# A hybrid encoder step on one core: handlers, squares and the last norm moved to other places

## Chip, core and metric

One core of a Trainium2 chip runs the kernel. The metric is the device time of one execution in microseconds (us). Engines are called TensorE (PE in rows; PEld its weight loads), VectorE (DVE), ScalarE (ACT), GpSimd (POOL) and SyncE (SP, which only issues transfers).

## The reference

One inference step of a one-layer encoder trunk, on 512 new frames and 32 frames of a running stream, 544 columns in all, with 2048 channels:

```python
# x: 544 rows of 2048, handled transposed in the kernel
z = rmsnorm(x, g_mix) @ w_in                       # 6152 wide: gb, gc, hin, q, k, v, 8 gates
yc = gb * short_conv(gc * hin)                     # width 3, over time
ya = forgetting_attention(q, k, v, cumsum(log_sigmoid(gates)))      # 8 heads of 128
x += concat(rmsnorm(yc, g_conv_out), rmsnorm(ya, g_attn_out)) @ w_out
x += cross_attention(rmsnorm(x, g_xattn), memory)  # 4 heads, 256 memory tokens
x += square(relu(rmsnorm(x, g_mlp) @ w_up)) @ w_down                # hidden 8192
y = rmsnorm(x, g_final)
```

The new keys, values, gates, last convolution rows and memory keys and values are returned too. All of it is fp32. A matrix product is made of three products of rounded parts: each operand is split into a high and a low half (`split`: ScalarE writes the rounded high half, VectorE subtracts for the low one), and hi x hi, hi x lo and lo x hi are added up in PSUM.

## The kernel before

Everything is channel-major: a tile holds 128 channels by 544 columns, `TH` = 272 being one half of the columns. The program is written in Python against a tile framework, which orders each engine's instructions at build time. It goes by priority, which is the place in the program, and takes at each moment of its own timing model the first instruction that is ready. `tc.high_priority(offset=n)` lifts instructions by n places; weight splits (`operand`) and sums of weight blocks (`combine`) are lifted by `AHEAD` = 40. Each engine and each queue then works in that fixed order. A tile comes from a pool with a number of buffers per tag, and an allocation waits until a buffer is free.

Large products use a seven-product scheme on 2x2 blocks (`class Seven`, run by `seven`): for a pair of 128-channel output tiles, four raw weight blocks a11, a12 (tag "raw", 3 buffers) and a21, a22 (tag "raw2", 4 buffers) are loaded, VectorE forms s1 = a21 + a22, s2 = s1 - a11, s4 = a12 - s2 and s3 = a11 - a21 (tag "sum", 3 buffers), and seven products of 24 matmuls each follow in the order b11, t1, t2, b22, t3, b21, t4. t2 is added onto what b11 left in PSUM, after ScalarE has copied that out (L280). The tags "hi" and "lo" have four buffers of 512 columns each, two products' worth. With `late=2` (first pair of a stage) b11 and t1 do the first six channel blocks, then the last two each. `fetch` loads a pair's blocks, `prefetch` the next pair's. `between` is called after t2.

The stages around the change, in order of time:

- **Head** (to 58 us). For j = 0 to 7, two x tiles are loaded (`xr`, L363) and a block of first weights (L364); ScalarE scales x by the gain (L367), `operands` makes the split operands (kept in `xops`), and 48 matmuls (L378) add to four output tiles hr0, gc0, gb0, hr1. `square` squares each x tile on ScalarE and adds it to `acc_x` on VectorE (L189, L163).
- **First norm and gates.** `rstd` sums the squares over channels by a matmul with 1/D (L178, name ssq), takes Ln and Exp on ScalarE and one Newton step in four VectorE instructions (L181 to L184). It is lifted by 150. `emit_logf` does 80 gate matmuls (L418). The four first tiles are scaled by the norm (L557) and given to their handlers: `on_hr` keeps the tile, `on_gc` forms u = gc * hr and the three-tap convolution (L502 to L512), `on_gb` multiplies by the gate, splits, stores and squares (L518, L88, L189). `evac_logf` scales the gates (z16).
- **Projection pairs** (70 to 540 us). Each pair of tiles goes through `seven`; the first tile's handler runs after b21 (`mid`), the second one's after the pair (`done`); a gb tile as second is held until the next pair's `between` (`release`). A gate step follows each of the first six pairs.
- Attention, output projection and cross-attention (540 to 912 us). In these `tmp` tiles (tag "t", 6 buffers of 548 columns) serve as scratch.
- **The MLP's entry** (912 to 992 us). For 16 tiles in the order 0, 8, 1, 9, ... the output of cross-attention is added to x2 (a `tmp` tile reloaded from DRAM), the sum is stored, squared by ScalarE (L1085) and added to one of two accumulators by a copy that accumulates, issued by POOL (L1086), and made into operands. The squares lie in "raw2" buffers, those of the last pair of tiles in `tmp`. Then come 32 pairs of w_up. The norm is applied after the product (`relu`, needing `rb_3`), and is made in `between` of the first pair.
- Down projection, and at the end (`a` = 0, 1: the halves of the columns) eight blocks of last weights each, the final sums, squares, gain, `rstd`, one multiplication per output pair (`finish`, VectorE) and stores, alternately from ScalarE's and SP's queues. The first half's outputs are finished during the second half.

## Time and profile before

| | us |
|---|---|
| median of 3 runs (2349.14 to 2350.31) | 2350.08 |
| the profiled execution | 2352.74 |
| its span, first to last instruction | 2351.0 |
| TensorE busy in it | 2312.8 |
| VectorE busy | 1999.7 |
| ScalarE busy | 1300.0 |
| POOL busy | 212.2 |

The profile is of one execution. Busy time of TensorE is that of pipelined matmuls, whose ends are modelled. Idle time before an instruction is put down to what released it. Starts are us from the start of the span.

### The profile page before, as it was taken

The page shows a single profiled execution, that of the slowest core. Times are in us where ns is not written, and L with a number is a line of the kernel's source. Part 1 is how long each engine was busy: PE and PEld are TensorE (multiplying, and loading weights), DVE is VectorE, ACT ScalarE, POOL GpSimd, SP SyncE. Part 2 cuts the span into 40 slices and gives each one's busy share as a digit, 9 for nine tenths or more (in the row PEclk, how much of TensorE's full clock was granted, in tenths as well). Part 3 has the DMA queues.
Part 4 walks back from the last instruction along what each step waited for, and adds up shares of the span by engine and source line. Part 5 has one row for each costly group of instructions (what it writes and reads, how often), then busy time and mean ns, then how long its engine had stood idle before and what let it go on. Part 6 is the DMA issues. An engine that isn't in the chain of part 4 may idle for free.

```text
span 2351.0 us, 47516 instructions
## 1 busy us (share of the span) xinstructions
PE 2312.8 (98%) x18151; PEld 2285.0 (97%) x18151; DVE 1999.7 (85%) x3546; ACT 1300.0 (55%) x2524; POOL 212.2 (9%) x402
## 2 busy tenths in 40 slices
PE   8999999999999999899999999999999999999997
PEld 8999999999999998799999999999999999999997
DVE  9999988877767757889999999998598888888887
ACT  8455555555644546556666566665255555555555
POOL 0000011114200001111111111111000000000000
PEclk9999999999999999999999999999999999999999
DMA  5333345578435537656565566556946636645523
GB/s 177 127 121 122 122 156 160 160 243 300 141 100 154 157 107 212 200 162 204 191 199 180 193 201 196 188 185 226 344 148 241 211 125 233 228 141 191 184 90 131
DMA packets 161861, 420.25 MB, mean 179 GB/s; under 512 B 19096, under 2 KB 23888, under 8 KB 161632
## 3 DMA queue, kind: packets, MB, share of 16 engines
q1 hardware_dynamic: 109888, 313.54, 39.8%
q0 software_dynamic: 46240, 94.75, 13.1%
q10 hardware_dynamic: 5504, 8.93, 1.1%
q8 instruction: 142, 2.33, 0.4%
q14 instruction: 87, 0.71, 0.1%
HBM read 319.91 MB, written 93.33 MB: 176 GB/s over the span
## 4 chain that ended last, share of the span: by engine, by line
PE 94%; DMA 2%; DVE 2%; ACT 1%; issue 1%; DVEq 0%; ACTq 0%; SPq 0%; POOLq 0%
PE mmx L271 27%; PE dx L1233 14%; PE mmy L271 14%; PE mm L120 13%; PE mm L1233 11%; PE mmz L271 7%; PE mm L1327 2%; PE mm L378 1%; PE h L378 1%; PE mm L914 1%; PE s L644 1%; DMA acc<-sq 1%; DMA raw<-in_w_ends 1%; DVE wlo L85 1%; DMA f<-fd 1%
## 5 line engine op out<-in xcount | busy, mean ns | idle before, releaser
L84 ACT ACTIVATE whi<-raw 128x512 fp32r<-128x512 f32 x664 | 417.8, 631 | 493.9 <-PE mmx L271 97.9
L84 ACT ACTIVATE whi<-sum 128x512 fp32r<-128x512 f32 x652 | 407.5, 630 | 418.6 <-PE mmx L271 186.2
L85 DVE TENSOR_TENSOR wlo<-raw,whi 128x512 fp32r<-128x512 f32 x664 | 453.3, 687 | 129.2 <-ACT whi L84 121.6
L85 DVE TENSOR_TENSOR wlo<-sum,whi 128x512 fp32r<-128x512 f32 x652 | 436.7, 684 | 70.3 <-ACT whi L84 65.9
L271 PE MATMUL mmx<-oph,whi 128*128 128x272 f32 x1296 | 372.8, 288 | 2.3 <-ACT h L280 2.2
L271 PE MATMUL mmx<-oph,wlo 128*128 128x272 f32 x1296 | 374.0, 289 | 0.1
L271 PE MATMUL mmx<-opl,whi 128*128 128x272 f32 x1296 | 371.5, 287 | 0.0
L1233 PE MATMUL dx<-f,whi 128*128 128x272 f32 x1792 | 344.4, 288 | 0.0
L1233 PEld LDWEIGHTS dx<-f,whi 128*128 128x128 f32 x1792 | 281.5, 188 | 0.0
L1233 PE MATMUL mm<-f,whi 128*128 128x272 f32 x1344 | 258.6, 288 | 0.0
L1233 PE MATMUL dx<-f,wlo 128*128 128x272 f32 x896 | 258.4, 288 | 0.0
L271 PE MATMUL mmy<-oph,whi 128*128 128x272 f32 x864 | 249.8, 289 | 7.6 <-ACT whi L84 7.6
L271 PE MATMUL mmy<-oph,wlo 128*128 128x272 f32 x864 | 249.9, 289 | 0.0
L271 PE MATMUL mmy<-opl,whi 128*128 128x272 f32 x864 | 248.9, 288 | 0.0
L271 PEld LDWEIGHTS mmx<-oph,whi 128*128 128x128 f32 x1296 | 244.0, 188 | 3.1 <-ACT h L280 2.6
L271 PEld LDWEIGHTS mmx<-oph,wlo 128*128 128x128 f32 x1296 | 243.3, 188 | 0.5 <-DVE wlo L85 0.5
L271 PEld LDWEIGHTS mmx<-opl,whi 128*128 128x128 f32 x1296 | 243.5, 188 | 0.0
L1233 PEld LDWEIGHTS mm<-f,whi 128*128 128x128 f32 x1344 | 210.6, 188 | 0.0
L1233 PE MATMUL mm<-f,wlo 128*128 128x272 f32 x672 | 193.4, 288 | 0.0
L271 PEld LDWEIGHTS mmy<-oph,whi 128*128 128x128 f32 x864 | 163.4, 189 | 8.1 <-ACT whi L84 8.0
L1233 PEld LDWEIGHTS dx<-f,wlo 128*128 128x128 f32 x896 | 168.9, 189 | 0.0
L271 PE MATMUL mmx<-b,whi 128*128 128x272 f32 x864 | 166.1, 289 | 0.1
(393 smaller groups left out, 5161.5 us busy)
## 6 DMA issues: line engine op xcount, KB each, us to landing
raw<-in_w_up SPq DMA_DIRECT2D x128, 512.0 KB, 3.9
raw<-in_w_dn SPq DMA_DIRECT2D x112, 512.0 KB, 4.4
f<-fd SPq DMA_DIRECT2D x196, 272.0 KB, 5.7
fd<-form POOLq DMA_DIRECT2D x168, 272.0 KB, 4.2
raw<-in_w_in SPq DMA_DIRECT2D x88, 512.0 KB, 3.8
raw<-in_w_out SPq DMA_DIRECT2D x32, 512.0 KB, 4.2
raw<-in_w_ends SPq DMA_DIRECT2D x20, 512.0 KB, 4.2
kq<-hl POOLq DMA_DIRECT2D x32, 256.0 KB, 3.3
```

The source lines that it names most:

```text
L84: act.activation(hi, src, AF.Copy)
L85: dve.tensor_tensor(lo, src, hi.bitcast(F32), ALU.subtract)
L120: pe.matmul(ps[a], w, two(x)[:, a], start=first and n == 0, stop=last and n == 2)
L271: pe.matmul(ps, a[:, c], x, start=first and j == 0 and n == 0, stop=j == 7 and n == 2, skip_group_check=not first)
L378: pe.matmul(ps[a], w[:, c], xs[a][q], start=j + i == 0 and n == 0, stop=j + i == 8 and n == 2)
L644: pe.matmul(s[:, :N], q[a][:, c], k[b][:, :N], start=n == 0, stop=n == 2)
L914: pe.matmul(ps[:, 0, :NMEM], w[:, c], x, start=k == 0 and n == 0, stop=k == KD - 1 and n == 2)
L1233: pe.matmul(ps, a[:, c], f[:, x], start=first and j == 0 and n == 0, stop=j == 3 and n == 2, skip_group_check=not first)
L1327: pe.matmul(ps, w[:, c], two(x)[:, a], start=k == 0 and j == 0, stop=k == 3 and j == 2)
```

## The change

Five things are done.

1. The head asks for the first weight block ahead of the first two x tiles, loads the gate weights `wf` at once on ScalarE's queue, and scales the first x tile on VectorE instead of ScalarE. From the second step on the squares of x are added by accumulating copies from POOL's queue into two accumulators; the first step's squares are written there by ScalarE.
2. The first norm and the four handlers (`begin`) are called in `between` of the first pair instead of ahead of it; `rstd` is no longer lifted, and takes an output tile. The gate steps come one pair later. The last gb tile is held for the next pair like the others.
3. The scratch pool has seven buffers instead of six. It now also holds `wf_hl`, the sample attention's `Ps` and `PTs`, and `xsP`.
4. At the MLP's entry the squares of the last three pairs of tiles (j > 4), instead of the last one, lie in the scratch pool, and `rb_3` is made after b22 (`behind`) instead of after t2.
5. The final norm (`last_rstd`) takes the last square without adding it to the accumulator first, as a second matmul, uses three dependent VectorE instructions instead of four after Exp, and leaves its result in PSUM. For the second half, POOL multiplies three of the eight output pairs, from a copy in SBUF; for the first half the norm is made one block later.

```diff
-    tpool = ctx.enter_context(tc.tile_pool(name="tmp", bufs=6))
+    tpool = ctx.enter_context(tc.tile_pool(name="tmp", bufs=7))
-    def rstd(acc, dim, width=T, early=0):
+    def rstd(acc, dim, width=T, out=None):
         accs = acc if isinstance(acc, list) else [acc]
-        with tc.high_priority(offset=early):
-            rt = npool.tile([128, T], F32, tag="rstd", name="rstd", bufs=3)
+        with tc.high_priority(offset=0):
+            rt = out if out is not None else npool.tile([128, T], F32, tag="rstd", name="rstd", bufs=3)
...
-    def seven(pl, ops, ws, out, scale, mid, prefetch, between=None, late=0):
+    def seven(pl, ops, ws, out, scale, mid, prefetch, between=None, late=0, behind=None):
...
         s.b22()
+        if behind:
+            behind()
         s.t3()
...
-    acc_x = new_acc()
+    acc_x = [new_acc(), new_acc()]
...
+    wf = headp.tile([128, KD, 8], F32, name="wf")
+    act.dma_start(wf, w_f)
...
         xr = [headp.tile([128, T], F32, tag="xr", name="xr", bufs=5) for i in range(2)]
+        if j == 0:
+            hi, lo = weights(w_first[j])
         for i in range(2):
             sp.dma_start(xr[i], xT[j + 8 * i])
-        hi, lo = weights(w_first[j])
+        if j:
+            hi, lo = weights(w_first[j])
...
-            act.activation(x[:, 2 * i:2 * i + 2], two(xr[i]), AF.Identity, scale=gain(G_MIX, j + 8 * i))
+            if j + i == 0:
+                dve.tensor_scalar(x[:, :2], two(xr[i]), gain(G_MIX, 0), None, ALU.mult)
+            else:
+                act.activation(x[:, 2 * i:2 * i + 2], two(xr[i]), AF.Identity, scale=gain(G_MIX, j + 8 * i))
...
-            square(xr[i], acc_x, j + i == 0)
+            if j:
+                sq = tmp("sq")[:, :T]
+                act.activation(sq, xr[i], AF.Square)
+                pool.dma_start(acc_x[i], sq, accum_op=ALU.add)
+            else:
+                act.activation(acc_x[i], xr[i], AF.Square)
...
-    rb = rstd(acc_x, D, early=150)
+    rb = npool.tile([128, T], F32, tag="rstd", name="rb", bufs=3)
     rbs = npool.tile([128, T], F32, tag="rstd", name="rbs", bufs=3)
-    dve.tensor_scalar(rbs, rb, SCALE, None, ALU.mult)
...
+    def begin():
+        rstd(acc_x, D, out=rb)
+        for t, (n, j) in enumerate((("hr", 0), ("gc", 0), ("gb", 0), ("hr", 1))):
+            dve.tensor_tensor(first_tiles[t], first_tiles[t], rb, ALU.mult)
+            kinds[n][1](j, first_tiles[t])
+        box["z"] = evac_logf(ps)
+        dve.tensor_scalar(rbs, rb, SCALE, None, ALU.mult)
...
-        nxt = seven(pj, xops, nxt, out, scale, mid, ahead, release, 2 if i == 0 else 0)
+        nxt = seven(pj, xops, nxt, out, scale, mid, ahead, release if i else begin, 0 if i else 2)
         done(i, out[1])
-        if i < len(steps):
-            steps[i]()
+        if 1 <= i <= len(steps):
+            steps[i - 1]()
         if pairs[i][1] == ("gb", 7):
-            release()
-            keep_cm.__exit__(None, None, None)
...
-        st.P = P = rp.tile([128, LS], F32, tag="Ps", name="Ps")
+        st.P = P = tmp("Ps")[:, :LS]
...
-            sq = (tmp("sq") if j == 7 else up.tile([128, 1024], F32, tag="raw2", name="sq", bufs=4))[:, :T]
+            sq = (tmp("sq") if j > 4 else up.tile([128, 1024], F32, tag="raw2", name="sq", bufs=4))[:, :T]
...
-                    lambda: fetch_up(i + 1), (lambda: rb_3.append(rstd(acc_3, D))) if i == 0 else None,
-                    2 if i == 0 else 0)
+                    lambda: fetch_up(i + 1), None, 2 if i == 0 else 0,
+                    (lambda: rb_3.append(rstd(acc_3, D))) if i == 0 else None)
...
+    def last_rstd(accs):
+        ps = aux("ssq")[:, :TH]
+        for n, t in enumerate(accs):
+            pe.matmul(ps, inv[D], t, start=n == 0, stop=n == len(accs) - 1)
...
+        act.activation(r0, ps, AF.Ln, bias=eps)
+        dve.tensor_scalar(v, ps, EPS, -0.5, ALU.add, ALU.mult)
+        act.activation(r0, r0, AF.Exp, scale=-0.5)
+        dve.tensor_tensor(q, r0, r0, ALU.mult)
+        dve.tensor_tensor(q, q, v, ALU.mult)
+        r = aux("r")[:, :TH]
+        dve.scalar_tensor_tensor(r, q, 1.5, r0, ALU.add, ALU.mult)
+        return r
...
-        rb_4 = rstd(acc_4, D, TH)
+        sums = [acc_4[:, :TH], sq_4]
+    rb_4 = last_rstd(sums)
+    rb_5 = tmp("rb")[:, :TH]
+    act.activation(rb_5, rb_4, AF.Copy)
     for p in range(8):
-        store(p, 1, finish((1, p), rb_4))
+        store(p, 1, finish((1, p), rb_5 if p in (2, 4, 7) else rb_4, pool if p in (2, 4, 7) else dve))
```

## Rows read from the trace of the kernel before

**Rows 1.** From the page, its first part: busy us of each engine, its share of the span, and the number of instructions.

```profile
PE 2312.8 (98%) x18151; PEld 2285.0 (97%) x18151; DVE 1999.7 (85%) x3546; ACT 1300.0 (55%) x2524; POOL 212.2 (9%) x402
```

**Rows 2.** A table of stretches. Columns: the stretch and its length; busy us and number of instructions of PE, PEld, DVE, ACT and POOL; the clock granted to TensorE as a share of full speed; the busy share of the 16 DMA engines; GB/s.

```profile
7.09:14.57 7.48, 7.48 (x38) 7.32 (x39) 7.43 (x22) 7.06 (x14) 0.00 (x0) 1.00 0.82 309
14.57:58.60 44.03, 44.00 (x346) 43.26 (x345) 43.58 (x82) 38.16 (x74) 0.00 (x0) 1.00 0.45 142
...
69.95:81.20 11.25, 9.76 (x76) 9.36 (x76) 11.25 (x18) 4.82 (x10) 1.22 (x2) 1.00 0.37 120
81.20:102.20 21.00, 21.00 (x165) 20.11 (x163) 19.63 (x38) 10.44 (x19) 0.00 (x0) 1.00 0.32 110
102.20:300.00 197.80, 197.00 (x1569) 196.40 (x1568) 186.16 (x321) 102.04 (x185) 10.04 (x19) 1.00 0.36 119
540.00:700.00 160.00, 159.98 (x1206) 151.02 (x1205) 117.92 (x364) 88.93 (x226) 34.55 (x64) 1.00 0.50 168
...
957.80:964.20 6.40, 0.10 (x2) 0.05 (x1) 1.95 (x3) 0.78 (x3) 1.72 (x2) 0.81 0.88 238
964.20:977.20 13.00, 8.28 (x38) 6.77 (x38) 9.56 (x15) 5.79 (x13) 0.00 (x0) 0.70 0.64 189
977.20:992.20 15.00, 15.00 (x120) 15.00 (x121) 14.18 (x26) 8.24 (x16) 0.00 (x0) 1.00 0.21 72
...
2341.50:2351.00 9.50, 0.00 (x0) 0.00 (x0) 4.41 (x7) 0.00 (x0) 0.00 (x0) 0.50 0.69 235
```

**Rows 3.** The timeline at the start of the span: start, us, engine, line, operation, out<-in, shapes, count, and in brackets the idle time ahead and what ended it.

```profile
1.15 0.30 POOL masks.py:199 TENSOR_SCALAR_AFFINE_SELECT ident<-ident 128x128 f32<-128x128 f32 x1
...
3.82 1.51 ACT L367 ACTIVATE x<-xr,vec 128x544 f32<-128x544 f32 x2 [1.33 <-DMA vec<-in_vecs]
...
7.09 1.50 PE L378 MATMUL mm<-b,whi 128*128 128x272 f32 x5 [7.09 <-ACT whi L84]
...
12.78 0.72 DVE L163 TENSOR_TENSOR acc<-acc,sq 128x544 f32<-128x544 f32 x1
...
13.69 0.65 ACT L189 ACTIVATE sq<-xr 128x544 f32<-128x544 f32 x1
```

**Rows 4.** The chain of work that ended last, in order of time, in the stretch 0 to 130: start, us, what, count.

```profile
58.63 1.16 PE ssq L178 x4
...
60.16 9.79 PE mm L418 x80
...
83.96 3.02 PE mmx L271 x24
```

**Rows 5.** What TensorE waited for between 60 and 540, all of it: us in total, times, longest.

```profile
PE mmx L271 <- ACT h L280: 2.2, 2, 1.5
```

**Rows 6.** VectorE's groups of instructions between 59.9 and 78, shapes kept apart: line, engine, operation, names, shapes, count, then busy us, mean ns of one, and idle us before them.

```profile
L557 DVE TENSOR_TENSOR hr<-hr,rstd 128x544 f32<-128x544 f32 x2 | 1.4, 717 | 0.0
L181 DVE TENSOR_TENSOR nt<-rstd 128x272 f32<-128x272 f32 x2 | 0.8, 439 | 0.8 <-ACT rstd L180 0.8
L511 DVE SCALAR_TENSOR_TENSOR y<-u,vec,y 128x546 f32<-128x546 f32 x1 | 0.8, 781 | 0.0
L88 DVE SCALAR_TENSOR_TENSOR ych<-gb,vec,ych 128x544 fp32r<-128x544 f32 x1 | 0.8, 778 | 0.0
L502 DVE TENSOR_TENSOR u<-gc,hr 128x512 f32<-128x512 f32 x1 | 0.7, 682 | 0.0
L183 DVE TENSOR_SCALAR nt<-nt 128x272 f32<-128x272 f32 x2 | 0.5, 290 | 0.0
L510 DVE TENSOR_SCALAR y<-u,vec 128x546 f32<-128x546 f32 x1 | 0.5, 499 | 0.0
L503 DVE TENSOR_TENSOR u<-gc,hr 128x32 f32<-128x32 f32 x1 | 0.2, 183 | 0.0
```

**Rows 7.** VectorE's timeline in the first pair, a run of low halves (columns as in rows 3).

```profile
77.48 2.48 DVE L85 TENSOR_TENSOR wlo<-sum,whi 128x512 fp32r<-128x512 f32 x4
```

**Rows 8.** The timeline at the MLP's entry, first TensorE's three waits, then VectorE's (columns as in rows 3).

```profile
964.15 0.60 PE L271 MATMUL mmy<-oph,whi 128*128 128x272 f32 x1 [6.30 <-ACT whi L84]
...
968.33 2.18 PE L178 MATMUL ssq<-acc,inv 128*128 128x272 f32 x4 [3.35 <-DMA acc<-sq]
...
977.17 0.39 PE L271 MATMUL mmy<-oph,whi 128*128 128x272 f32 x1 [1.27 <-ACT whi L84]
...
962.15 1.23 DVE L232 TENSOR_TENSOR sum<-raw,raw 128x1024 f32<-128x1024 f32 x1 [5.76 <-DMA raw<-in_w_up]
```

**Rows 9.** Transfers at the MLP's entry. First what SP's queue waited for from 930 to 965 (us in total, times, longest); then POOL's queue from 905 to 985 (packets, MB, share of the 16 engines' time); POOL's issues of accumulating copies (busy us, mean ns of one | idle before); and how long these took from issue to landing.

```profile
SPq L222 <- DMA acc<-sq: 8.2, 3, 6.2
...
q0 software_dynamic: 2016, 3.90, 28.7%
...
L1086 POOL DMA_DIRECT2D acc<-sq x14 | 12.1, 863 | 51.5 <-ACT sq L1085 28.7 <-DMA acc<-sq 13.4 <-ACT oph L84 7.7
...
DMA to landing us min/median/max: 4.0/6.7/8.2
```

**Rows 10.** The chain that ended last, after the last matmul: start, us, what.

```profile
2336.73 0.45 DVE acc L163
...
2337.99 0.50 ACT rstd L179
...
2339.93 0.31 DVE nt L183
```

More of the change, by code (lines that the diff above doesn't have):

```diff
@@ L190, in square @@
         accumulate(acc[:, cols], sq[:, cols], first)
-    wf = cpool.tile([128, KD, 8], F32, name="wf")
-    wf_hl = cpool.tile([128, KD, 16], F32R, name="wf_hl")
     sel16 = cpool.tile([16, 8], F32, name="sel16")
@@ L551, in fetch_pair @@
         return fetch(pj, w_in, *(kinds[n][0] + j for n, j in pairs[i]), last)
-    steps = (lambda: gate_open(z16), gate_exp, gate_log, gate_close, gate_sum, turn_logf)
-    ps = emit_logf()
-    nxt = fetch_pair(0)
-    for t, (n, j) in enumerate((("hr", 0), ("gc", 0), ("gb", 0), ("hr", 1))):
-        dve.tensor_tensor(first_tiles[t], first_tiles[t], rb, ALU.mult)
-        kinds[n][1](j, first_tiles[t])
-    z16 = evac_logf(ps)
     held = []
@@ L564, in release @@
             held.pop()()
+    steps = (lambda: gate_open(box["z"]), gate_exp, gate_log, gate_close, gate_sum, turn_logf)
+    ps = emit_logf()
+    nxt = fetch_pair(0)
+    box = {}
+    def begin():
[5 more added lines that the diff above has]
+        dve.tensor_scalar(rbs, rb, SCALE, None, ALU.mult)
     def job(i):
@@ L732, in samp_transpose @@
         pt = aux("pts")
-        PT = pl.tile([128, 3, 128], F32, tag="PTs", name="PTs")
+        PT = tmp("PTs")[:, :384].rearrange("p (a b) -> p a b", a=3)
         n = L // 128
@@ L1024, in xs_scores @@
         mx = xp.tile([128, 3], F32, name="xsmx")
-        P = xp.tile([128, NMEM], F32, name="xsP")
+        P = tmp("xsP")[:, :NMEM]
         dve.tensor_reduce(mx[:, 0:1], s[:, :NMEM], axis=AX.X, op=ALU.max, negate=True)
@@ L1286, in hybrid_step, with finish @@
     fin = {}
-    def finish(p, r):
+    def finish(p, r, eng):
         y = fin.pop(p)
-        dve.tensor_tensor(two(y), two(y), r[:, :TH].unsqueeze(1).to_broadcast([128, 2, TH]), ALU.mult)
+        eng.tensor_tensor(two(y), two(y), r.unsqueeze(1).to_broadcast([128, 2, TH]), ALU.mult)
         return y
+    def last_rstd(accs):
+        ps = aux("ssq")[:, :TH]
+        for n, t in enumerate(accs):
+            pe.matmul(ps, inv[D], t, start=n == 0, stop=n == len(accs) - 1)
+        r0 = npool.tile([128, T], F32, tag="rstd", name="r0", bufs=3)[:, :TH]
+        v, q = (tmp(n)[:, :TH] for n in ("v", "q"))
+        act.activation(r0, ps, AF.Ln, bias=eps)
[6 more added lines that the diff above has]
+        return r
     def store(p, a, y):
@@ L1329, in hybrid_step @@
                 dve.tensor_tensor(xa, xa, ps, ALU.add)
-                square(xa, acc_4, n == 0 and i == 0, slice(0, TH))
+                if n == 7 and i == 1:
+                    sq_4 = tmp("sq")[:, :TH]
+                    act.activation(sq_4, xa, AF.Square)
+                else:
+                    square(xa, acc_4, n == 0 and i == 0, slice(0, TH))
                 act.activation(two(y)[:, i], xa, AF.Identity, scale=gain(G_FIN, m))
-            if a and n:
-                store(n - 1, 0, finish((0, n - 1), rb_4))
+            if a and n == 0:
+                rb_4 = last_rstd(sums)
+            elif a:
+                store(n - 1, 0, finish((0, n - 1), rb_4, dve))
         if a:
-            store(7, 0, finish((0, 7), rb_4))
-        rb_4 = rstd(acc_4, D, TH)
+            store(7, 0, finish((0, 7), rb_4, dve))
+        sums = [acc_4[:, :TH], sq_4]
+    rb_4 = last_rstd(sums)
+    rb_5 = tmp("rb")[:, :TH]
+    act.activation(rb_5, rb_4, AF.Copy)
     for p in range(8):
-        store(p, 1, finish((1, p), rb_4))
+        store(p, 1, finish((1, p), rb_5 if p in (2, 4, 7) else rb_4, pool if p in (2, 4, 7) else dve))
     down_cm.__exit__(None, None, None)
```

5 lines of the change are left out of this document (3 added, 2 removed).

## The prediction

> **What bounds the kernel now.** I read the page first: TensorE is busy for 98% of the span [rows 1], so a gain can only come from its idle time, 38 us in all. A table of stretches shows where that lies: 7.1 us before its first matmul [rows 3], 1.5 us near 76, 0.8 us between 102 and 300, 6.3 and 4.7 us on either side of 964, and the end of the span [rows 2]. The other thing to see in that table is VectorE: it is busy 11.25 of 11.25 us around the gap at 76 and for 94% of the time up to 300. In the input projection it is the next engine to bind, so what is moved onto it there is soon paid for. Then I read each gap for itself: the timeline at the start [rows 3], the chain around 76 [rows 4], TensorE's waits in the projection [rows 5], the MLP's entry [rows 8, 9] and the end [rows 10].
>
> **First loads reordered.** Today ScalarE scales two x tiles from 3.82 (1.5 us), rounds two halves and the first weights, and TensorE begins at 7.09 [rows 3]. Afterwards the weights are asked for ahead of x, so ScalarE can round them early, and VectorE scales the first x tile (0.50 us, as L510 in [rows 6]). But x then lands behind 0.5 MB more, 1.7 us at 309 GB/s [rows 2]; some of it is hidden, since x has to wait for the gains until 3.8 anyhow. I take x at 5.0, scaled at 5.5, rounded at 6.2, first matmul at 6.4: -0.7 us. Bounds: -1.9 (x as early as now) and +0.3 (ScalarE takes the second x tile ahead of the rounding).
>
> **Head squares by accumulating copies.** VectorE loses 16 additions of 0.72 us [rows 3]. But TensorE ran 346 matmuls in 44.0 us there [rows 2], at 0.126 us each when nothing is late (24 in 3.02 us [rows 4]), so at most 0.5 us is to be had. Against it stand 14 accumulating copies on POOL's queue. At the MLP's entry the same 14 took 28.7% of the 16 DMA engines' time in 80 us, 1.64 us each, and they form chains: issue 0.86, landing 6.7 in the median and 8.2 at most [rows 9]. Two chains of seven links of 7.6 us start at 14.3, the end of the second step's first square [rows 3], and end near 67.5. The sum of squares will be asked for near 77 (75.97 less 1.2 and 0.7, and one product of 3.0). So 9.6 us cover it; seven of the longest links, 9.1, would end at 78. Taken: 0; bounds -0.5 and +11 (a link of 10.5 us, below).
>
> The Trainium skill speaks against this edit: by DMA: Bandwidth & Descriptors, section "Issuing engines are not separate DMA queues", copies issued by POOL run on the same 16 DMA engines as those of SP and ACT, so that a further queue adds no room. By that rule 23 us of accumulating copies come on top of the loads' 20 us (share 0.45 of 44 us), 43 of 44, and links would be long, which is the third rival below. The trace agrees in so far as the share was 0.88 where both kinds ran together [rows 2].
>
> **Two accumulators.** The sum takes eight matmul records where four took 1.16 us [rows 4]: +1.2 us, on TensorE itself.
>
> **First channel tiles' handlers moved behind the third product of the first pair.** Removed: the wait of 1.5 us near 76. ScalarE was busy with handler output and weights while TensorE waited for its copy L280 [rows 5]; without the handlers that copy runs at once: -1.5 us (0 if something else is there).
>
> Moved: one burst of VectorE work. By the durations of [rows 6]: rstd's Newton steps 2 x (3 x 0.44 + 0.29) = 3.2; four scalings and z16, 5 x 0.72 = 3.6; u and the gate product with their 32-column rests 2 x (0.68 + 0.18) = 1.7; four small ones, under 0.18 each, 0.7; the taps 0.50 + 2 x 0.78 = 2.1; a low half 0.8; a copy and rbs, as L510, 1.0. That is 13.1 us in 27 instructions, each starting some 0.08 us before the one ahead ends (four low halves of 0.68 us take 2.48 [rows 7]), so 11.0. It used to run between 60 and 77, where TensorE had 9.8 us of gate matmuls to do [rows 4]. There VectorE will now idle, and it can't work far ahead, since four hi and four lo tiles hold two products.
>
> Let T0 be the end of the third product. TensorE does 2.3 us of sums and then the two products that are already split, 3.0 each: fed until T0 + 8.3. The sixth product's tiles come free from T0 + 3.8 on, but its split stands 58 instructions behind the burst's end and is lifted by 40 only, so VectorE does the burst first. It begins at T0 + 2.2 (first sums 1.2, two ScalarE steps of 0.5 as at the end [rows 10]), ends at T0 + 13.2, and the first low tile takes 0.7 more. TensorE, after two matmuls that need no low tile, waits from T0 + 8.6 to T0 + 13.9, 5.3 us; some of the next pair's sums can be done ahead, so I take **+5**. Bounds: 0 (the split is placed ahead of the handlers) and +11 (nothing absorbed, for VectorE has only 1.4 us idle in the pair that follows [rows 2]). What is late next is the sixth product and all behind it in the pair.
>
> The last gate tile's handler no longer runs at once beside another. Of TensorE's two waits for L280 in the projection, 2.2 us together [rows 5], the second, 0.7, falls there: -0.7 (0 to -0.7).
>
> **The MLP's entry.** TensorE waits 6.30 us for weights, because VectorE's sum of two raw blocks waited 5.76 for a transfer [rows 8], which SP could issue only when copies of squares had freed the raw2 buffers (three waits, 8.2 us [rows 9]). In the new kernel the squares from the sixth pair of tiles on lie in the scratch pool, so raw2 comes free with earlier copies and the blocks can land by 955. Then TensorE waits 3.35 for the accumulating copies, as the norm's sum stands ahead of the second product; it is now placed one product (3.0 us) later. Then 1.27. Together 10.9 us, and some 2 us more, as the granted clock was 0.70 in the mean of that stretch [rows 2].
>
> Not all of it returns. VectorE had no idle time before 956.4 (962.15 less 5.76), and still has to do the raw sum and its low halves (1.2 + 1.3), the last tiles' operands (5 x 0.72 + 3 x 0.44 = 4.9), s2 and its low halves (2.5). So the second product begins near 959 and the third near 966; that one, the fourth, the sums and three more (5 x 3.0 + 2.3) end the pair at 983.5, against 992.2 now (its last 120 matmuls fill the stretch from 977.2 [rows 2]): 8.7. The scratch pool, seven buffers for reloads and six squares, can make a reload 1 to 2 us late. I take **-8**; bounds -12 and -1.
>
> **The end.** The last square's addition (0.45) and one of four Newton steps (0.31) leave the chain [rows 10]: -0.8. One more sum for the first half's norm: +0.3. The stores run at a DMA share of 0.69 over 9.5 us, the fill and the last landing included [rows 2], 8 x 272 KB in a stream; so products shared with POOL gain nothing unless they hold the stream up. No POOL multiply is in this trace: its nearest row, 0.30 us for 128 columns [rows 3], makes 1.3 for 544; VectorE's, 0.72. Together -0.5, bounds -0.8 and +0.4.
>
> The rest (guests in the scratch pool, wf by ScalarE's queue at once, gate steps one pair later) I cost at nothing: in the attention stage TensorE is busy for 159.98 of 160 us [rows 2], and the seventh buffer stands in for the guests. Without that cover a late guest costs TensorE one low half, 0.7.
>
> **Sum.** -0.7 + 0 + 1.2 - 1.5 + 5 - 0.7 - 8 - 0.5 = **-5.2 us**. The profiled execution took 2352.74 us (span 2351.0 and 1.7 around it), 0.11% above the median of the runs, 2350.08. So 2347.5 on its scale and 2344.9 on the median's: **2345 us**.
>
> **The rivals.** First: the burst costs nothing, as the build puts the sixth product's split ahead of the handlers. VectorE's 13 us of idle pieces from 81 to 300 [rows 2] would hold it; against it, those pieces are waits for buffers. -10.2: 2340 us. Second: the entry's wait only changes its name, as the norm's sum is again pulled ahead on TensorE's queue, as before [rows 8], and the copies' chain ends no earlier. Then 2 of the 8 us are gained: 2351 us. Third, slower, by one mechanism: the head's loads and accumulating copies fill the DMA engines. A link over 9.0 us makes TensorE wait at T0 seven times the excess; the gain is gone at 9.7, and at 10.5 the wait is 10.7: 2355.6 us. For it, 8.2 + 0.9 was seen; against it, the median, 7.6.
>
> **How the numbers follow.** My forecast 0.45, the rivals 0.25, 0.2 and 0.1. A measurement of this kernel tells 0.2% (4.7 us) from no change. Faster than 2345.4: the first rival and half of my forecast, 0.48. Within: the other half and most of the second, 0.40. Slower than 2354.8: the third and a remnant, 0.12. The range 2338 to 2353 takes in the first two rivals; left out are the third and the ends where all bounds fall together, 2334 and 2373.
>
> **What would show it.** A first matmul near 6.4, no wait for loads in the head, and the last accumulating copy landed before the sum. No wait near 76, and instead, some 8 us after the third product, about 5 us for a low half with VectorE full. At the entry raw sums before 957, waits under 5 us in place of 10.9, a granted clock near 1. At the end 0.8 us less from last matmul to first store. I am wrong if VectorE shows slack behind the burst, or if the norm's sum still stands ahead of the second product.

## The result, and the profile after

The changed kernel takes 2355.76 us in the median (2353.12 to 2359.58), beside 2351.07 for the kernel before: ratio 1.0019, 95% interval 1.0011 to 1.0027. It is 4.7 us slower (2.6 to 6.3) where 5.2 us less were forecast. Its profiled execution took 2354.01 us with a span of 2352.0; before it was 2352.74 and 2351.0. These two single executions differ by 1.3 us, less than the medians, so below a term is read from a stretch of the trace and checked on the medians of kernels that have one part alone or one part undone. Either reading is good to about 1 us. One execution each of entry_alone, sum_in_old_place, direct_sums and squares_on_vector was 6% to several times longer than its others; ranges and ratios leave it out. In the code after, L271, L280 and L289 are L269, L278 and L287; the head's matmuls are L386, the gate matmuls L430.

The stretches that answer to [rows 2] (same columns, the changed kernel):

```profile
7.09:14.57 7.48, 6.52 (x39) 6.42 (x40) 7.17 (x23) 7.42 (x16) 0.00 (x0) 1.00 0.98 331
14.57:58.60 44.03, 43.46 (x347) 43.24 (x345) 36.86 (x70) 38.81 (x78) 12.26 (x14) 1.00 0.97 238
69.95:81.20 11.25, 11.25 (x85) 10.91 (x85) 7.72 (x10) 6.16 (x13) 0.00 (x0) 1.00 0.10 40
81.20:102.20 21.00, 16.82 (x126) 15.75 (x125) 21.00 (x51) 8.21 (x15) 1.11 (x2) 1.00 0.24 78
...
957.80:964.20 6.40, 2.72 (x19) 2.36 (x17) 3.27 (x6) 3.27 (x6) 0.86 (x1) 0.95 1.06 351
964.20:977.20 13.00, 10.76 (x57) 9.74 (x56) 10.71 (x16) 8.38 (x17) 1.72 (x2) 0.76 0.57 144
977.20:992.20 15.00, 13.75 (x109) 13.75 (x110) 14.50 (x28) 7.60 (x15) 0.00 (x0) 1.00 0.41 139
```

Three things are to be seen. The gap of 1.5 us in 69.95:81.20 is gone, and VectorE idles there. In the next stretch VectorE is busy for 21.00 of 21.00 us and TensorE does 126 matmuls where it did 165: 39 fewer, 4.9 us at 0.126. Four of the 165 were gate sums (1.0 us), which the changed kernel does later; with these counted apart the burst costs 5.2 us. And at the MLP's entry TensorE is idle for 7.2 us (3.68, 2.24 and 1.25 in the three stretches), where it was idle for 11.0; the granted clock is still 0.76 in the middle one.

What TensorE waited for in the changed kernel from 0 to 300 (us in total, times, longest):

```profile
PE mm L386 <- ACT b L84: 8.1, 1, 8.1
PE mm L430 <- ACT hr L410: 1.1, 1, 1.1
...
PE mmx L269 <- DVE wlo L85: 2.9, 2, 2.3
PE mmx L269 <- ACT h L278: 0.9, 1, 0.9
```

The first row is the start: 8.1 us, where it was 7.1. The second is new. Before, the norm's four sums ran between the head's last matmul and the gate matmuls (1.16 us, [rows 4]) and covered the time in which ScalarE still copied the head's PSUM tile. The sums were moved away, so TensorE stands. The last two rows are the burst.

The start after, which answers to [rows 3]:

```profile
4.77 1.15 ACT L84 ACTIVATE whi<-raw 128x512 fp32r<-128x512 f32 x2 [2.29 <-DMA raw<-in_w_first]
...
5.43 1.29 DVE L85 TENSOR_TENSOR wlo<-raw,whi 128x512 fp32r<-128x512 f32 x2 [5.43 <-ACT whi L84]
5.82 0.64 ACT L394 ACTIVATE acc<-xr 128x544 f32<-128x544 f32 x1
6.61 0.75 ACT L375 ACTIVATE x<-xr,vec 128x544 f32<-128x544 f32 x1
6.64 0.50 DVE L373 TENSOR_SCALAR x<-xr,vec 128x544 f32<-128x544 f32 x1
7.27 0.73 ACT L84 ACTIVATE b<-x 128x272 fp32r<-128x272 f32 x2
```

VectorE takes the two low halves of the weights (1.29 us) ahead of the x tile that TensorE wants; ScalarE takes a square (0.64) and the second x tile (0.75) ahead of the rounding. The x tile was scaled at 7.1 and not at 5.5.

The timeline at the entry to the MLP after, which answers to [rows 8], ScalarE and VectorE first, then TensorE:

```profile
959.60 0.66 ACT L1102 ACTIVATE sq<-x2r 128x544 f32<-128x544 f32 x1 [3.93 <-issue]
...
960.93 0.72 DVE L205 TENSOR_TENSOR ts<-x 128x544 f32<-128x544 f32 x1 [3.71 <-ACT x L1106]
...
963.57 0.58 PE L269 MATMUL mmy<-oph,whi 128*128 128x272 f32 x1 [3.68 <-ACT whi L84]
965.51 0.82 PE L269 MATMUL mmx<-b,whi 128*128 128x272 f32 x2 [1.13 <-DVE x2r L1095]
...
978.45 0.39 PE L269 MATMUL mmy<-oph,whi 128*128 128x272 f32 x1 [1.97 <-ACT whi L84]
```

And the one accumulating copy that POOL issued at 950.94, from issue to landing:

```profile
DMA to landing us min/median/max: 8.6/8.6/8.6
```

ScalarE's square of the fourteenth tile stands for 3.93 us, VectorE behind it for 3.71, TensorE behind that for 3.68. "Issue" means that the profile knows no releaser; but in the program a square has to wait until its scratch buffer is free, and the copy issued at 950.94 still reads an older square from one. 950.94 and 8.6 make 959.5. That this copy is the cause is shown in the experiments. The blocks that the prediction wanted earlier did come earlier (issued at 946.54 and 948.24, 8.8 us to landing): they lay there while VectorE stood.

### The profile page after: what moved, and what is told of

Same layout as the page of the kernel before. It is cut to its first block, busy times and chain, and to the rows that moved or that the text cites. A ratio compares the mean times of both kernels' runs of the same rounds, so it can differ in the third digit from the quotient of the medians.

```text
span 2352.0 us, 47564 instructions
## 1 busy us (share of the span) xinstructions
PE 2313.2 (98%) x18159; PEld 2285.8 (97%) x18159; DVE 1990.5 (85%) x3526; ACT 1299.3 (55%) x2524; POOL 227.8 (10%) x419
## 4 chain that ended last, share of the span: by engine, by line
PE 94%; issue 3%; DVE 2%; ACT 0%; DMA 0%; POOLq 0%; POOL 0%; SPq 0%; DVEq 0%; ACTq 0%
PE mmx L269 27%; PE dx L1250 14%; PE mm L120 14%; PE mmy L269 14%; PE mm L1250 11%; PE mmz L269 7%; PE mm L386 1%; PE h L386 1%; PE mm L931 1%; PE mm L946 1%; PE s L661 1%; PE o L717 1%; PE pt L695 0%; PE mm L430 0%; DVE wlo L85 0%
## 5 line engine op out<-in xcount | busy, mean ns | idle before, releaser
L269 PE MATMUL mmx<-oph,wlo 128*128 128x272 f32 x1296 | 374.1, 289 | 2.3 <-DVE wlo L85 2.3
L269 PE MATMUL mmx<-oph,whi 128*128 128x272 f32 x1296 | 372.8, 288 | 1.3 <-ACT h L278 0.9
L269 PE MATMUL mmx<-opl,whi 128*128 128x272 f32 x1296 | 371.5, 287 | 0.0
L269 PE MATMUL mmy<-oph,whi 128*128 128x272 f32 x864 | 250.0, 289 | 6.3 <-ACT whi L84 5.7
L269 PE MATMUL mmy<-oph,wlo 128*128 128x272 f32 x864 | 249.4, 289 | 0.2 <-DVE wlo L85 0.2
L269 PE MATMUL mmy<-opl,whi 128*128 128x272 f32 x864 | 248.9, 288 | 0.0
L269 PEld LDWEIGHTS mmx<-oph,wlo 128*128 128x128 f32 x1296 | 243.3, 188 | 2.7 <-DVE wlo L85 2.7
L269 PEld LDWEIGHTS mmx<-oph,whi 128*128 128x128 f32 x1296 | 244.0, 188 | 1.9 <-ACT h L278 1.1
L269 PEld LDWEIGHTS mmx<-opl,whi 128*128 128x128 f32 x1296 | 243.5, 188 | 0.0
L269 PEld LDWEIGHTS mmy<-oph,whi 128*128 128x128 f32 x864 | 163.1, 189 | 7.2 <-ACT whi L84 6.1
L269 PE MATMUL mmx<-b,whi 128*128 128x272 f32 x864 | 168.0, 291 | 1.6 <-DVE x2r L1095 1.1
```

The lines of the kernel that those rows point to most:

```text
L269: pe.matmul(ps, a[:, c], x, start=first and j == 0 and n == 0, stop=j == 7 and n == 2, skip_group_check=not first)
```

## The experiments

All times are medians of 5 to 12 executions; ratios are to the kernel before on the same chip. Four chips were used, and the kernel before took 2350.9 to 2351.9 on them, so a difference of under 1 us between two medians shows nothing by itself.

**The burst.** *handlers_first* is the changed kernel with the handlers back ahead of the first pair:

```
-        nxt = seven(..., ahead, release if i else begin, ...)
+    rb = rstd(acc_x, D, early=150); ...; for t, (n, j) in ...: scale, kinds[n][1](j, first_tiles[t])
+        nxt = seven(..., ahead, release, ...)
```

The gate steps and the last gate tile go back to their old places with it.

> The changed kernel, with the first four channel tiles' handlers, the norm behind them and the gate steps put back ahead of the first pair; all else as changed. Theory A (the burst of VectorE work is the largest loss): between 88.9 and 100.2 TensorE's matmuls start 5.4 us late in all, beside the gate sums that moved; the wait of 1.5 us near 76 and the one of 0.7 near 291 come back. Net 3.2 us faster than the changed kernel, 2352.5 against 2355.8. Rival B (the burst takes the place of idle time that is lost anyway, so that moving it back only moves the wait): within 1 us of the changed kernel, 2355 to 2357.

Measured: 2351.03, ratio 1.0000 (0.9992 to 1.0009), 4.7 us faster than the changed kernel: theory A, with 1.5 more than it said. What TensorE waited for in it from 0 to 300:

```profile
PE mm L386 <- ACT b L84: 8.3, 1, 8.3
PE mmx L269 <- ACT h L278: 1.1, 2, 0.7
PE mmx L269 <- DVE wlo L85: 0.2, 1, 0.2
```

The wait near 76 came back with 0.4 us only, not 1.5, since VectorE is free of the head's squares (squares_alone, below, has the same 0.4); and the wait ahead of the gate matmuls is gone, as the sums cover it again. Both were missing in the expectation.

*pool_scalings* is the changed kernel with four of the burst's products on GpSimd:

```
-            dve.tensor_tensor(first_tiles[t], first_tiles[t], rb, ALU.mult)
+            pool.tensor_tensor(first_tiles[t], first_tiles[t], rb, ALU.mult)
```

> The changed kernel with the four scalings of the first channel tiles done by GpSimd instead of VectorE, so that the burst has 2.6 us less VectorE work. Theory A (TensorE's wait behind the third product is the burst's VectorE time and nothing else): the waits of 5.4 us shrink by 2.6, the kernel is 2.6 us faster than the changed one (2355.8), 2353.2. Rival B (VectorE works in the order of its queue and stands for GpSimd's slower products before the gate product): no gain or up to 2 us slower, 2355.5 to 2358.

Measured: 2359.20, ratio 1.0034 (1.0022 to 1.0047): rival B, and 1 us more than it said. VectorE's and POOL's timelines in it:

```profile
84.65 2.04 POOL L579 TENSOR_TENSOR hr<-hr,rb 128x544 f32<-128x544 f32 x1 [30.55 <-DVE rb L184]
86.65 1.36 POOL L579 TENSOR_TENSOR gc<-gc,rb 128x544 f32<-128x544 f32 x1
87.97 1.36 POOL L579 TENSOR_TENSOR gb<-gb,rb 128x544 f32<-128x544 f32 x1
89.28 1.78 POOL L579 TENSOR_TENSOR hr<-hr,rb 128x544 f32<-128x544 f32 x1
...
88.05 1.83 DVE L514 TENSOR_TENSOR u<-gc,hr 128x512 f32<-128x512 f32 x1 [2.24 <-POOL gc L579]
89.80 1.31 DVE L515 TENSOR_TENSOR u<-gc,hr 128x32 f32<-128x32 f32 x1
```

VectorE stands for 2.24 us, and then its products take 1.83 and 1.31 us beside GpSimd's, where the changed kernel has 0.69 and 0.19 for the same two. TensorE's longest wait behind the burst grew from 2.3 to 3.9 us, and after it the granted clock was 0.51 from 97 to 104, where the changed kernel had 1.00; that is part of the loss.

*one_handler* takes the kernel with direct sums (below) and moves one handler, gb, instead of four:

```
+        if n == "gb": held.append(lambda: first(2, "gb", 0))   # runs behind the third product
```

> The kernel with direct sums (2344.1), with one of the first four channel tiles' handlers (gb: some 4.4 us of VectorE work) moved behind the third product of the first pair and the others left ahead of the pair. Theory A (TensorE has two split products and the sums ahead of it, so the burst of 13.1 us cost 5.4 and one below 7.7 costs nothing): no new wait near 90, and of the wait of 1.5 us near 76 at least half goes: 2342.6 to 2343.5. Rival B (what is moved onto VectorE there is paid for in full): 3 us slower, 2347.

Measured: 2343.29 beside 2344.09 for its base, too little to tell by the medians; the trace shows theory A. TensorE's waits from 60 to 300 are one of 0.7, where its base has 2.0 in two. The moved piece is 2.8 us of VectorE (0.71, 0.68, 0.18, 0.78, 0.44), not the 4.4 of the expectation, which counted taps that belong to gc.

**The MLP's entry.** *entry_alone* is the kernel before with `bufs=7`, `j > 4`, the guests in the scratch pool and `behind`:

> The kernel before with the MLP entry's edits alone: seven scratch buffers and the guests in them (the gate weights' split too), the last six squares in the scratch pool, the norm's sum one product later. Theory A (the trace after shows what the edit is worth: ScalarE's square at 959.6 waits 3.9 us for a scratch buffer that an accumulating copy still holds, so that part of the entry's wait only moved): 3.4 us faster than the kernel before, 2347.7. Rival B (the prediction's price; the other edits delay the entry in the changed kernel): 8 faster, 2343. Rival C (the entry gains nothing in most executions, as transfers of 8 to 11 us there leave it to chance): 2350 to 2352.

Measured: 2349.50, ratio 0.9990 (0.9981 to 0.9999); by the trace 3.4 us gained between 946 and 985. Theory A, though the median gained 2.0 where it said 3.4. Its square of the fourteenth tile, and the copy issued at 947.09:

```profile
955.49 0.66 ACT L1087 ACTIVATE sq<-x2r 128x544 f32<-128x544 f32 x1 [4.20 <-issue]
...
DMA to landing us min/median/max: 8.3/8.3/8.3
```

947.09 and 8.3 make 955.4.

*sum_in_old_place* is the same with `between` for `behind`:

> The kernel before with the MLP entry's edits, except that the norm's sum stays ahead of the fourth product, as before. Theory A (the sum's place is worth its wait for the last copies): a wait of some 3 us for the copies stands in front of the sum again; 2 to 3 us slower than with all of the entry's edits (2349.5), 2351.5 to 2352.5. Rival B (the place is worth nothing: on TensorE's queue the sum is pulled ahead in both, and what counts are the buffers): 2349 to 2350.

Measured: 2349.40, ratio 0.9997 (0.9987 to 1.0006). By the median the moved sum is worth nothing, by the ratio up to 1.6 us, and the intervals of the two kernels overlap; in the trace no wait stands ahead of the sum: rival B. On TensorE's queue the sum stands behind most of the first two products in both; it runs at 968.1 and 968.8. The square of the fourteenth tile here, and the copy issued at 946.27:

```profile
954.53 0.66 ACT L1087 ACTIVATE sq<-x2r 128x544 f32<-128x544 f32 x1 [3.25 <-issue]
...
DMA to landing us min/median/max: 8.2/8.2/8.2
```

*direct_sums* leaves six accumulating copies out and lets TensorE sum these squares:

```
             act.activation(sq, x, AF.Square)
-            pool.dma_start(acc_3[i], sq, accum_op=ALU.add)
+            if j > 4: late_sq.append(sq)   # two tiles later: pe.matmul(ssq[n], inv[D], sq half n)
+            else: pool.dma_start(acc_3[i], sq, accum_op=ALU.add)
```

> The kernel before with the MLP entry's edits alone, and with one more: the last six squares are not added up by accumulating copies; TensorE takes each of them straight into the norm's sum, two tiles later (twelve more records of 0.23 us). Theory A (the entry's remaining wait is a scratch buffer that an accumulating copy holds: ScalarE's square, and the reload behind it, stand for 3.9 us): that wait goes, and with it 9.8 us of all 16 DMA engines' time. First wait of the entry under 1 us in place of 3.9; 3 to 4 us faster than the entry's edits alone (2349.5), 2345.5 to 2346.5. Rival B (the DMA engines are full there with loads and stores anyway, so the raw blocks land no sooner and TensorE waits for their sum instead): 2349 to 2350.

Measured: 2344.09, ratio 0.9971 (0.9961 to 0.9982), 5.4 us faster than entry_alone. Two stretches of it:

```profile
957.80:964.20 6.40, 6.40 (x50) 6.10 (x48) 5.84 (x10) 4.96 (x9) 0.00 (x0) 1.00 0.25 96
964.20:977.20 13.00, 12.25 (x84) 11.26 (x84) 13.00 (x21) 7.61 (x15) 0.00 (x0) 1.00 0.27 87
```

and all that TensorE waited for in it from 935 to 1000:

```profile
PE mmy L270 <- DVE opl L85: 0.8, 1, 0.8
```

The entry's waits are down to 0.8 us and the granted clock stays at the upper of its two levels, where entry_alone had 0.58 and 0.94 in the same stretches. The gain is larger than theory A's 3 to 4 us; the clock is part of what it left out.

This kernel takes away both the buffers' hold and the copies' DMA time. *copies_elsewhere* was to part the two, with copies of the same size from another tile:

```
-            pool.dma_start(acc_3[i], sq, accum_op=ALU.add)
+            if j < 5: pool.dma_start(acc_3[i], sq, accum_op=ALU.add)
+        if j > 4: pool.dma_start(acc_3[i], b11s[-1].bitcast(F32), accum_op=ALU.add)
```

> The kernel before with the MLP entry's edits alone, except that the last six accumulating copies read an operand tile that is there anyway in place of the squares (so the sum of squares is left out for these six tiles; all squares are still computed, and as many copies of the same size run). It takes the copies' hold on the scratch buffers away and leaves their DMA time. Theory A (the buffers are the wait): ScalarE's square waits for no copy, the entry's first wait of 3.9 us falls under 1, 3 to 4 us faster than the entry's edits alone (2349.5): 2345.5 to 2346.5. Rival B (the copies' share of the DMA engines is the wait: loads land late because of them): the wait moves to the sum of the raw blocks or to the reloads and stays near 4 us; 2349 to 2350.

Measured: 2356.47, ratio 1.0024, against the times of both theories. But the mechanism is A's: no square waited for a buffer, though the first three of the six copies took 7.4 to 8.9 us to land, and the entry's first wait, 3.9 us in entry_alone, was gone. Only, the build now put the norm's sum ahead of nearly all of the first pair's products, and there TensorE waited for the copies:

```profile
954.50 0.39 PE L270 MATMUL mmy<-oph,whi 128*128 128x272 f32 x1
...
966.03 2.18 PE L178 MATMUL ssq<-acc,inv 128*128 128x272 f32 x4 [11.02 <-DMA acc<-b]
```

So the run doesn't part the two by its time, and the copies were issued up to 4 us earlier or later than in entry_alone, which weakens it. It shows the next thing in line: as long as copies add up the squares, their two chains end at 966.0 and 968.6 (entry_alone: 966.4 and 968.4), and whatever is queued behind the sum pays for that.

*direct_four* parts them better. It is direct_sums with `j > 5`: two more copies than direct_sums (3.3 us of DMA time).

> The kernel with direct sums (2344.1), with four squares instead of six taken straight into the norm's sum; the two of the sixth pair go by accumulating copy again. Theory A (each square summed on TensorE costs its two records, 0.46 us, and two of them less free 0.9): 2343.2, if the two copies, landed by about 955, hold no buffer that is wanted. Rival B (any copy from the scratch pool stands in the way of the last reloads or squares): a wait of 1 to 3 us comes back, 2344 to 2346.

Measured: 2347.81, ratio 0.9985 (0.9976 to 0.9994), 3.7 us slower than direct_sums: rival B, and 1.8 us more than it said at most. One square and TensorE's wait behind it, from the timeline:

```profile
954.31 0.66 ACT L1097 ACTIVATE sq<-x2r 128x544 f32<-128x544 f32 x1 [3.40 <-issue]
...
960.21 0.82 PE L270 MATMUL mmx<-b,whi 128*128 128x272 f32 x2 [3.26 <-DVE x2r L1090]
```

and the accumulating copy that POOL issued at 946.15:

```profile
DMA to landing us min/median/max: 8.1/8.1/8.1
```

946.15 and 8.1 make 954.2; the square runs at 954.31. Four kernels (the changed one, entry_alone, sum_in_old_place, direct_four) show the same: the square starts 0.07 us behind the landing of the copy that holds its buffer. That is the cause of the entry's remaining wait. Stores and loads that landed near it lie 0.3 to 1.4 us off, differently in each kernel. How much of the copies' 8 us is the load of the DMA engines wasn't measured by itself.

**First loads.** *loads_as_before* undoes the order in the changed kernel, *loads_alone* does it alone in the kernel before:

```
+        if j == 0: hi, lo = weights(w_first[j])   # ahead of xr
+            if j + i == 0: dve.tensor_scalar(x[:, :2], two(xr[i]), gain(G_MIX, 0), None, ALU.mult)
```

> The changed kernel with the first loads in the old order (x ahead of the weights) and both first x tiles scaled by ScalarE. Theory A (the later first matmul costs nothing in the end, since TensorE's clock goes up sooner: 0.96 us late at the first matmul, 0.2 early at 13 us): first matmul near 7.1, and within 0.5 us of the changed kernel, 2355.3 to 2356.3. Rival B (the start is a loss of its full 1 us): 2354.8.

> The kernel before with the first loads reordered alone (weights ahead of x, the first x tile scaled by VectorE). The prediction's price was -0.7. Theory A (x lands later and stands behind VectorE's low halves and ScalarE's second x tile): first matmul between 8.0 and 8.6 instead of 7.1; 0.9 slower in the trace at 40 us, 2352 in the median. Rival B (TensorE's later start is given back, as its clock goes up at a time that does not hang on the first matmul): under 0.3 at 40 us, 2351.

Measured: 2354.70 (1.1 faster than the changed kernel) and 2352.56 (ratio 1.0005, 0.9996 to 1.0013). The first matmul came at 7.9 and at 8.2. In the new order the five traces have 8.1 to 8.3; in the old one twelve have 7.1 to 8.0, so a single trace could mislead by the size of the term. Both runs lean to a loss of about 1 us (rival B for loads_as_before, theory A for loads_alone), and neither proves it by the median. In all of them the first matmuls run at the lower of the clock's two levels (0.23 to 0.30 us each, as in [rows 3]; 0.126 later on) for another 3.1 to 6.0 us; the changed kernel's profiled execution had one of the short ones (3.3, where the kernel before had 5.8), which hid its later start. The trace's record of the clock begins only at 11.3 and 12.9 in these two, where the slow matmuls end, so the 1.00 in the rows of 7.09:14.57 does not speak against it.

**Head squares.** *squares_on_vector* undoes the copies in the changed kernel, *squares_alone* makes them in the kernel before:

```
-            square(xr[i], acc_x, j + i == 0)
+            sq = tmp("sq")[:, :T]; act.activation(sq, xr[i], AF.Square)
+            pool.dma_start(acc_x[i], sq, accum_op=ALU.add)      # two accumulators
```

> The changed kernel with the head's squares summed by VectorE into one accumulator again, so that no accumulating copy runs in the head and the norm's sum takes four matmul records instead of eight. Theory A (the copies filled the DMA engines, share 0.97, but TensorE waited for no load and the head got 0.7 us shorter; the second accumulator cost 0.9): 0.2 us faster, 2355.6, DMA share in the head back near 0.45. Rival B (with the DMA engines full the head differs from one execution to the next, and that is why the median of the changed kernel lies 1.7 us above its profiled execution and its runs spread over 6.5 us): 2 to 4 us faster, 2352 to 2354, with a spread like that of the kernel before. Rival C (the 16 additions put VectorE in front again): 1 us slower.

> The kernel before with the head's squares summed by accumulating copies into two accumulators, and nothing else; the norm's sum then stands ahead of the gate matmuls as before. The prediction's price was 0 for the copies and +1.2 for the second accumulator. Theory A (VectorE is freed: the head gets 0.7 shorter, the wait near 76 loses 1.1; the sum costs 0.9 more): 0.5 to 1 faster, 2350.5. Rival B (the sum is wanted at 58, earlier than in the changed kernel, and waits for the last copy, which landed near 59 there; DMA share 0.97): a wait of 1 to 3 us ahead of the sum, 2352 to 2353.

Measured: 2354.80 (1.0 faster than the changed kernel, spread 2352.6 to 2358.2) and 2352.41 (ratio 1.0008, 0.9999 to 1.0017). The first lies between theory A (2355.6) and rival B (2354 at most), within the error of either; the DMA share was back at 0.44, as A said, and B's smaller spread didn't show. In the trace of squares_alone the head ends 0.5 us sooner, the sums cost 1.0 more and the wait near 76 loses 1.1; no wait stands ahead of the sum, and so far A holds. The median lies on the other side, 0.6 us slower. The profiled execution (2356.33) lost much of it at the entry: TensorE waited 10.8 us there for weights, 6.3 in the kernel before, 5.3 in loads_alone, with the same instructions in the same order on every engine. So that wait differs from one execution to the next; whether it explains the median too isn't shown.

**The end.** *norm_alone* is the kernel before with the last norm's edits; *norm_plain* is direct_sums with them, but without ScalarE's copy of the result and with all products on VectorE:

```
-    rb_5 = tmp("rb")[:, :TH]; act.activation(rb_5, rb_4, AF.Copy)
-        store(p, 1, finish((1, p), rb_5 if p in (2, 4, 7) else rb_4, pool if p in (2, 4, 7) else dve))
+        store(p, 1, finish((1, p), rb_4, dve))
```

> The kernel before with the edits of the last norm and the last products alone. Theory A (read from the two traces: 15.6 us from the last matmul's start to the end before, 15.9 after, since the first product waits 0.9 us for ScalarE's copy of the result): 0.3 us slower, 15.9 us from the last matmul to the end again. Rival B (the prediction's -0.5; in the changed kernel another edit delays the end): 15.1 us. In the medians neither can be told from no change, 2350.5 to 2352; the trace decides.

> The kernel with direct sums (2344.1), with the changed kernel's last norm, but all products on VectorE from PSUM, without ScalarE's copy of the result and without GpSimd. Theory A (in the changed kernel the gain of the shorter norm went into the 0.9 us wait for the copy and into stores queued behind GpSimd's products): 14.7 us from the last matmul to the end in place of 15.6 before and 15.9 in the changed kernel; 2343.2. Rival B (the stores' stream sets the end by itself, so a first product 0.8 us sooner changes nothing): 15.6 us, 2344.

Measured: 2351.81 (ratio 1.0003) and 2343.42 (0.7 faster than its base); as expected, the traces have to decide. From the last addition to x until the end of the span it is 15.26 us before (2335.74 to 2351.0), 15.57 in the changed kernel and in norm_alone, 14.15 in norm_plain (15.5 in its base, direct_sums). The timeline of the end, of the kernel before:

```profile
2335.74 0.44 DVE L1329 TENSOR_TENSOR x<-x,mm 128x272 f32<-128x272 f32 x1
...
2341.49 0.38 ACTq L1295 DMA_DIRECT2D out_y<-yout  x1
```

of the changed kernel:

```profile
2336.43 0.44 DVE L1361 TENSOR_TENSOR x<-x,mm 128x272 f32<-128x272 f32 x1
...
2340.90 0.40 ACT L1377 ACTIVATE rb<-r 128x272 f32<-128x272 f32 x1 [1.47 <-DVE r L1322]
2341.33 3.25 DVE L1307 TENSOR_TENSOR yout<-yout,r 128x544 f32<-128x544 f32 x5 [0.46 <-ACT rb L1377]
2341.38 3.92 POOL L1307 TENSOR_TENSOR yout<-yout,rb 128x544 f32<-128x544 f32 x3 [690.96 <-ACT rb L1377]
2342.75 2.24 ACTq L1327 DMA_DIRECT2D out_y<-yout  x4
2345.32 2.46 SPq L1327 DMA_DIRECT2D out_y<-yout  x4
```

and of norm_plain:

```profile
2326.65 0.44 DVE L1363 TENSOR_TENSOR x<-x,mm 128x272 f32<-128x272 f32 x1
...
2330.84 5.14 DVE L1309 TENSOR_TENSOR yout<-yout,r 128x544 f32<-128x544 f32 x8
2331.59 4.17 ACTq L1329 DMA_DIRECT2D out_y<-yout  x4
```

In the changed kernel VectorE's first product waits 0.46 us for ScalarE's copy, and the first store of each queue is of a GpSimd product: the first of them ends 1.3 us after it begins, the third at 2345.30, when SP's queue starts. In norm_plain the first store comes 4.9 us after the last addition, in the changed kernel 6.3, and in the kernel before 5.8: without ScalarE's copy and GpSimd the 0.8 us of the prediction is there.

**Together.** The kernel before with the entry's edits and six direct sums, one handler moved, and the plain norm:

> The kernel before with what the runs showed to gain: the MLP entry's edits with six direct sums, one handler (gb) behind the third product of the first pair, and the last norm with all products on VectorE. If the gains stand in different stretches and add up: -0.8 and -0.7 on the direct sums' 2344.1, 2342.6, 0.36% below the kernel before. If one of them depends on the clock or on chance (the medians of both lay within 1 us of 2344.1): 2343 to 2344.

Measured: 2341.88 (2341.15 to 2343.98), ratio 0.9962 (0.9950 to 0.9975). That is 2.2 us below direct_sums where 1.5 were forecast, so the gains add up within the error; it beats both kernels.

## Why the prediction was wrong

Measured beside the terms of its sum, in us:

| term | predicted | measured |
|---|---|---|
| first loads | -0.7 | about +1 (medians of two runs); first matmul at 8.1 |
| head squares by copies | 0 | -0.5 at the head's end (squares_alone) |
| two accumulators | +1.2 | +1.0 (squares_alone) |
| gate matmuls wait for the PSUM tile | not seen | +1.1 |
| wait near 76 | -1.5 | -1.5 |
| burst behind the third product | +5 | +5.2 |
| wait near 291 | -0.7 | -0.7 |
| a wait for ScalarE's copy L287 at 190 | not seen | +0.6 |
| MLP's entry | -8 | -3.4 in the trace, -2.4 in the ratio (entry_alone) |
| the end | -0.5 | +0.3 |

The measured column makes +3.1 with the trace's reading of the entry, in the lower part of the result's interval. The medians of the kernels with one part alone or undone make +5.0, beside the 4.7 measured: first loads +1.1 (forecast -0.7), the head's squares with both accumulators +1.0 (+1.2), the handlers with all their waits +4.7 (+2.8), the entry -2.0 (-8), the end +0.2 (-0.5). The two accumulators and the two waits for L280 came as priced.

**The MLP's entry** is the step that failed, with 5 to 6 of the 8 us. Its first half was right: raw2 comes free earlier, the blocks land at 955 and 957, and the norm's sum no longer waits. The failed sentence is that the scratch pool "can make a reload 1 to 2 us late". A reload was late, by 2.4 us, but that was the smaller part. The sentence counted buffers and asked only who reloads into them. It didn't ask how long a copy holds its source, 7.4 to 8.6 us here (the prediction had 8.2 at most among its own rows), nor who writes next: ScalarE, in the order of its queue, with the operands of the last tiles behind it. The wait went from SP's queue, where it held loads, to ScalarE's, where it also held the operands, and VectorE behind them. That is near the second rival, a wait that changes its name, though by another one than it named. That nearly all of the 8 us were there to be had is shown by direct_sums, 7.5 us below the kernel before, though by another edit.

**The burst** came with the size forecast and by another way, so part of the agreement is luck. TensorE stopped 10.7 us behind T0 (78.5), not 8.6, and in the seventh product, not the sixth, since the build put two low halves (at 83.25 and 84.21) between the handlers, as the first rival had it for all. Then each further low half came late, at 90.70, 92.01 and 95.27, and the 5 us fell in several waits. That VectorE sets this is shown by handlers_first; the slack ahead of it, by one_handler.

**First loads**: x landing at 5.0 was wrong. Its two tiles landed at 5.6 and 6.5, behind the weights; before, the first landed at 3.6, and ScalarE was scaling both from 3.82 on. Besides, the work that was to fill the time (low halves, a square, the second x tile) stood ahead of x in both engines' queues. The upper bound, ScalarE taking the second x tile first, is what happened, and more.

**The new wait of 1.1 us** was missed because the sums were moved without asking what they hid. The prediction priced the sums where they went, not the hole where they had stood. The wait of 0.6 us at 190 was missed too; it is not in handlers_first, and which of the moves brings it wasn't tested.

**The third rival** had the share right and the price wrong. By the Trainium skill, DMA: Bandwidth & Descriptors, section "Issuing engines are not separate DMA queues", the copies run on the same 16 engines as the loads; the trace agrees, the share in the head rose from 0.45 to 0.97. But the links took 5.3 us in the median, 8.8 at most, the last was issued at 54.06, and TensorE waited for none.

**The end**: the chain lost its addition and its step as counted. The result's copy by ScalarE (0.40, and 0.46 of waiting) and the stores queued behind GpSimd's products took more than that back.

## What to carry to other kernels

A buffer is as long in use as its slowest reader: a pool is sized by the landing time of a copy in that very stretch, with the DMA engines as full as they are there, and the instruction that waits for it stalls all that its engine has queued behind. Before moving work out of a gap, look at what else used the gap as cover; and before moving it onto the busiest engine, work out how long its consumer is fed without it: a piece below that cost nothing here (2.8 us), and of one above it the excess was paid (5.2 us for a burst of 13 us of VectorE work). If a sum ends on TensorE anyway, its last terms are better taken there directly than by a copy that the sum then waits for.

## What the runs showed of the hardware

The time of an accumulating copy of 272 KB from issue to landing was 3.7 to 4.0 us at the entry's end, where the DMA share was 0.81 to 0.85, and 7.4 to 8.6 ahead of that, where it was 0.99 to 1.07 (the changed kernel). The share alone doesn't set it: in the head, at 0.97, it was 5.3 in the median.

VectorE's product of two SBUF tiles took 1.83 us instead of 0.69, and one of 32 columns 1.31 instead of 0.19, while GpSimd ran products of SBUF tiles (pool_scalings); GpSimd's own four took 2.04, 1.36, 1.36 and 1.78, and the third, at 1.36, ran beside VectorE's 1.83. In the last stage, where one operand of VectorE's products lies in PSUM, five of them took 3.25 us beside GpSimd's, 0.65 each. The Trainium skill, SBUF — State Buffer, section "Who interferes with whom", says this: a VectorE instruction with two SBUF inputs contends with a GpSimd instruction that reads SBUF; one with at most one SBUF input, outside the modes that use two ports, does not. The traces agree in both cases, with 1.83 and 1.31 us for the first and 0.65 for the second (0.64 in norm_plain, without GpSimd).
